# A gMLP and dilated-attention layer on one core: the keys of the stride-16 pattern put in block order where they are made

## The chip, the cores and the metric

The kernel runs on one core of a Trainium2 chip. The metric is the device time of one execution in microseconds (us). A core has a matrix engine (PE, its weight loads shown as PEld), a vector engine (DVE), a scalar engine (ACT), a general engine (POOL) and a queue engine (SP) that issues nearly all transfers here. Each engine works through its own list of instructions in order and waits on semaphores where a result of another engine is needed.

## The reference, cut to what matters

One layer over 2048 tokens of width 1024. A branch A (gated MLP with 128x128 position mixing) and a branch B (attention) are merged by gates and projected. The change touches branch B alone:

```python
DILATED_PATTERNS = ((128, 1), (512, 4), (2048, 16))      # window, dilation
# q, k, v: 16 heads of 64 columns, 2048 tokens
def to_blocks(t):        # L = S // dilation tokens per residue class, blocks of 128
    t = t.reshape(Bn, H, L, dilation, Dh).transpose(0, 1, 3, 2, 4)
    ...
s = jnp.einsum('bhrnqd,bhrnkd->bhrnqk', qb, kw) * (Dh ** -0.5)
...                      # ALiBi penalty, causal window, softmax over s, times v
o = num / sum(alphas)[..., None]       # the three patterns merged by their denominators
```

For dilation 16 there are 16 residue classes of 128 tokens each: query block b holds the tokens b, b+16, b+32 and so on, and attends only to the keys of the same class. The scores of a block are one 128x128 tile.

## The kernel before, in words

All large products are done in two or three parts of split precision: a high part and the rest (`hi`/`lo`, `whi`/`wlo`, `KH`/`KL`, `ph`/`pl`).

**Projections.** The tokens are taken in two halves of 1024 (`hf`), each in two quarters of 512 (`qds`). `unit_S` makes 1024 output columns in four rounds `m` of seven products (a Strassen scheme), with weights cast on ACT (line 83) and their low parts made on POOL (line 86), in a ring of eight tiles. The results of the products go through seven PSUM banks, taken in turn by `bank()`. In each round `evac` is called four times with a 128x512 tile of the result. For k and q that is `ev_qk`: ACT writes `qh` (line 448), DVE writes `ql` (line 449), and two transfers store them in `k_d` or `q_d` in DRAM, in token order. k is made first, then q, in each half.

**Attention.** `window` goes through 16 heads, in each through the patterns p = 2, 1, 0 (dilations 16, 4, 1), and in each pattern through four groups of four query blocks. `load_qk` brings the head's q, KH and KL from DRAM in token order. For p = 2 and p = 1 the columns are put in block order by `permuted`, a generator that is advanced three times per group and that finishes before the pattern it serves: while pattern 0 of head h runs, the keys and queries of pattern 2 of head h+1 are made. For p = 2 these are four copies `QP` on ACT, four `KHP` and four `KLP` on DVE (all line 614), each 128x512 with steps of 16 elements in the input; for p = 1 four `KHP` on DVE and four `KLP` on ACT (line 611).

A group has three stages. `stage_s`: score products (lines 654 and 655, K is the moving operand) into one of two PSUM tiles `ss`, then DVE adds the bias and takes the row minimum (line 662, output `S` and `ob`), then ACT takes the exponential (line 668). `stage_t`, two groups later: PE transposes the probabilities into one of three PSUM tiles `pt` (line 684), ACT writes the high part `ph` (687), DVE the rest `pl` (688). `stage_o`, three groups later: three products per pair with V (lines 701 to 703). After a head's last group `combine` merges its three patterns (DVE, POOL, some PE transposes at line 754), spread over the next head's groups.

Between these stages `run` advances `fill`, 80 units of other projections (line 103, tiles `pj`), so that PE has work while the attention waits. The build then orders the instructions of each engine by its own plan, within the dependences, so the order below is read from the built program.

Of the kernel before, what the change touches and what calls it, by code (L numbers as in the profile page):

```python
# [16 lines left out]
P = 128  # L17
# [10 lines left out]
class Prog:  # L28
# [8 lines left out]
    def setup(self):  # L37
        nc, tc, ctx, io = self.nc, self.tc, self.ctx, self.io
        self.const = c = ctx.enter_context(tc.tile_pool(name="const", bufs=1))
        self.ps = ctx.enter_context(tc.tile_pool(name="ps", bufs=1, space=bass.MemoryType.PSUM))  # L40
        dr = ctx.enter_context(tc.tile_pool(name="dr", bufs=1, space=bass.MemoryType.DRAM))
        self.xp = ctx.enter_context(tc.tile_pool(name="xp", bufs=1))
        self.wk = ctx.enter_context(tc.tile_pool(name="wk", bufs=2))
        self.gn = c.tile([P, KC], F32, name="gn")
        nc.scalar.dma_start(out=self.gn, in_=io["g_norm"])
        self.gv = c.tile([P, KC], F32, name="gv")
        nc.scalar.dma_start(out=self.gv, in_=io["g_v"])
        self.ident = c.tile([P, P], F32, name="ident")
        nc.scalar.dma_start(out=self.ident, in_=io["ident"])
        self.mhalf = c.tile([P, 8], F32, name="mhalf")  # L50
        nc.vector.memset(self.mhalf, -0.5)

        self.gmax = c.tile([P, 1], F32, name="gmax")
        nc.vector.tensor_reduce(out=self.gmax, in_=self.gn, axis=AX.X, op=ALU.max, apply_absolute_value=True)
        self.skq = c.tile([P, 16], F32, name="skq")
        self.sk, self.sq = self.skq[:, 0:8], self.skq[:, 8:16]
        self.sv = c.tile([P, 4], F32, name="sv")
        self.sqk = c.tile([P, 8], F32, name="sqk")
        self.niqk = c.tile([P, 8], F32, name="niqk")
        self.ihv = c.tile([P, 4], F32, name="ihv")  # L60

        self.q_d = [dr.tile([2, P, T], F16, name=f"q_d{i}") for i in range(NH // 2)]
        self.k_d = [dr.tile([2, P, T], F16, name=f"k_d{i}") for i in range(NH // 2)]
        self.v_d = [dr.tile([4, T, 130], F16, name=f"v_d{i}") for i in range(NH // 4)]
        self.ya_d = [dr.tile([D, 512], F32, name=f"ya_d{i}") for i in range(4)]
        self.yb_d = [dr.tile([D, 512], F32, name=f"yb_d{i}") for i in range(4)]
        self.bg_d = [dr.tile([D, 512], F32, name=f"bg_d{i}") for i in range(4)]
        self.ga_d = [dr.tile([D, 512], F32, name=f"ga_d{i}") for i in range(4)]
        self.gb_d = [dr.tile([D, 512], F32, name=f"gb_d{i}") for i in range(4)]
        self.ma_d = [dr.tile([D, 512], F32, name=f"ma_d{i}") for i in range(4)]  # L70
        self.av_d = [dr.tile([T // 2, D], F32, name=f"av_d{i}") for i in range(2)]
        self.o_d = [[dr.tile([T, 66], F32, name=f"o_d{h}_{p}") for p in range(2)] for h in range(NH)]
# [365 lines left out]
                        yield  # L438


    def ev_qk(self, dst, s):
        nc = self.nc

        def ev(nb, qd, ps):
            hi = self.wq.tile([P, 512], F16, name="qh", tag="qh")
            lo = self.wq.tile([P, 512], F16, name="ql", tag="ql")
            sc = s[:, nb:nb + 1]
            nc.scalar.activation(hi, ps, AF.Copy, scale=sc)
            nc.vector.scalar_tensor_tensor(out=lo, in0=ps, scalar=sc, in1=hi, op0=ALU.mult, op1=ALU.subtract)
            for part, t in ((0, hi), (1, lo)):  # L450
                nc.sync.dma_start(out=dst[nb][part][:, 512 * qd:512 * qd + 512], in_=t)
        return ev

    def ev_v(self, vp, hf):
# [41 lines left out]
    def branch_a(self, ap, hf, X):  # L496
        nc, io = self.nc, self.io
        mk = ap.tile([P, P], F32, name="mk", bufs=1)
        nc.sync.dma_start(out=mk, in_=io["causal"])
        ss = ap.tile([P, 8], F32, name="ss", bufs=1)  # L500
        rsv = ap.tile([P, 8], F32, name="rsv", bufs=1)
        nc.vector.tensor_reduce(out=ss, in_=self.ssv, axis=AX.X, op=ALU.add)
        self.rsqrt_mean(rsv, ss, 8)
        um, gr = {}, {}

        def group(g):
            av = ap.tile([P, 8, P], F32, name="avg", tag="avg", bufs=2)
            nc.sync.dma_start(out=av, in_=self.av_d[hf][:, g * P:(g + 1) * P].rearrange("(n p) d -> p n d", p=P))
            nc.vector.tensor_mul(av, av, rsv[:, :, None].broadcast_to([P, 8, P]))
            w = ap.tile([P, P], F32, name="wst", tag="wst")  # L510
            nc.sync.dma_start(out=w, in_=io["wsT"][:, g])
            nc.vector.tensor_mul(w, w, mk)
            b = ap.tile([P, P], F32, name="bsb", tag="bsb")
            nc.sync.dma_start(out=b, in_=io["bs"][:, g])
            return av, w, b

        def ev_u(g, qd, ps):
            q = qd % 2
            av, w, b = gr[g]
            u = um[g, qd] = ap.tile([P, 512], F32, name="um", tag="um", bufs=5)  # L520
            nc.scalar.activation(u, ps, AF.Gelu_apprx_tanh)
            px = self.pt()
            for i in range(4):
                nc.tensor.matmul(px[:, i * P:(i + 1) * P], av[:, 4 * q + i], w, start=True, stop=True)
            m = self.wk.tile([P, 512], F32, name="tm", tag="t5")
            nc.vector.scalar_tensor_tensor(
                out=m.rearrange("p (n t) -> p n t", n=4), in0=px.rearrange("p (n t) -> p n t", n=4),
                scalar=self.gv[:, g:g + 1], in1=b[:, None, :].broadcast_to([P, 4, P]), op0=ALU.mult, op1=ALU.add)
            nc.vector.tensor_mul(u, m, u)

        def ev_g(g, qd, ps):
            t = self.wk.tile([P, 512], F32, name="tg", tag="t5")
            nc.scalar.activation(t, ps, AF.Tanh, scale=0.5)
            nc.vector.scalar_tensor_tensor(out=t, in0=t, scalar=1.0, in1=ps, op0=ALU.add, op1=ALU.mult)
            nc.vector.scalar_tensor_tensor(out=t, in0=t, scalar=0.5, in1=um[g, qd], op0=ALU.mult, op1=ALU.mult)
            nc.sync.dma_start(out=self.ya_d[qd][g * P:(g + 1) * P], in_=t)

        qds = (2 * hf, 2 * hf + 1)
        gu = self.unit_S(X, io["w_in"], 0, ev_u, qds)
        gg = self.unit_S(X, io["w_in"], 2048, ev_g, qds)  # L540
        for g in range(2):
            gr[g] = group(g)
        yield
        for m in range(4):
            yield next(gu)
            for g in (2 * m + 2, 2 * m + 3):
                if g < 8:
                    gr[g] = group(g)
            yield next(gg)
# [66 lines left out]
            yield  # L616
        return r

    def permuted(self, at, raw, p):

        nc = self.nc
        Q, KH, KL = raw[:3]
        k = [Q.rearrange("p (n a q) -> p q n a", q=4, n=4)]
        if p == 2:
            r = yield from self.permute(at, nc.scalar.copy, Q, "QP", p, 1)
            k[0] = r.rearrange("p (b a) -> p b a", a=P)
        k.append((yield from self.permute(at, nc.vector.tensor_copy, KH, "KHP", p, 2)))
        k.append((yield from self.permute(at, nc.vector.tensor_copy if p == 2 else nc.scalar.copy, KL, "KLP", p, 2)))
        self.qkp[p] = k

    def stage_s(self, at, G):
# [14 lines left out]
        for i2 in range(2):  # L646
            ps = self.ps.tile([P, 2, 256], F32, name="ss", tag="ss", bufs=2)
            for i in range(2):
# [2 lines left out]
                n = 256 if prev else P  # L651
                q = Q[:, P * b:P * b + P] if p == 0 else Q[:, b // 4, b % 4] if p == 1 else Q[:, b]
                w = slice(P * (b + 1) - n, P * (b + 1))
                nc.tensor.matmul(ps[:, i, :n], q, KH[:, w], start=True, stop=False)  # L654
                self.pe = nc.tensor.matmul(ps[:, i, :n], q, KL[:, w], start=False, stop=True)  # L655
                rng.append(n)
            for i in range(2):
                j = 2 * i2 + i
# [103 lines left out]
    def window(self, at, fill, total_fill):  # L762
# [26 lines left out]
        for _ in range(24 // self.every * 2):  # L789
            self.seg(fill)  # L790
        raw = {0: self.load_qk(at, 0)}
        for _ in self.permuted(at, raw[0], 2):
            pass
        vt[0, 2] = self.load_v(at, 0, 2)
        for _ in range(24 // self.every * (ahead - 2)):
# [2 lines left out]
        for j in range(n + 3):  # L798
            if j < n:
# [14 lines left out]

                nxt = {2: (h, 1), 0: (h + 1, 2)}.get(p)
                if nxt and nxt[0] < NH and g == 0:
                    perm = self.permuted(at, raw[nxt[0]], nxt[1])
                next(perm, None)
            if 2 <= j < n + 2:
                run(self.stage_t(at, groups[j - 2]))  # L820
# [108 lines left out]
    def run(self):  # L929
# [5 lines left out]
        def drain(g):  # L935
            for _ in g:
                pass
# [4 lines left out]
        with pool("tp", bufs=1) as self.tp, pool("wr", bufs=2) as self.wr, pool("cp", bufs=1) as self.cp:  # L942
            X = [None, None]
            for hf in range(2):
# [27 lines left out]
                with pool(f"wq{hf}", bufs=2) as self.wq:  # L972
                    branch_a = self.branch_a(self.wq, hf, X)
                    next(branch_a)
                    for c0, dst, sc in ((4096, self.k_d, self.sk), (3072, self.q_d, self.sq)):
                        drain(self.unit_S(X, win, c0, self.ev_qk(dst, sc), qds))
                    drain(branch_a)
                if hf == 0:
                    drain(self.unit_S(X, win, 6144, self.ev_bg, qds))
# [70 lines left out]
```

## Time and profile before

| | us |
|---|---|
| median of 3 runs | 2652.31 (2652.05 to 2658.41) |
| the profiled execution | 2664.8, span of its instructions 2663.0 |
| PE busy in the span | 2497.5 |
| DVE busy | 1835.0 |
| ACT busy | 1261.1 |
| POOL busy | 886.1 |

The mean granted clock of PE in the profiled execution is 0.982 of full speed. Three stages matter here. k is made from 245 to 327 us (first half of the tokens) and from about 1000 to 1085 us (second half). The attention window runs from about 1335 to 2285 us. After it comes a final projection. A matmul's shown duration includes its way through the array: matmuls overlap, so PE's busy time is longer than its work and its idle time is shorter than what it lost.

### The profile page before, as it was taken

What the parts mean: (1) busy time and instruction counts of PE and PEld (TensorE: products, weight loads), DVE (VectorE), ACT (ScalarE), POOL (GpSimd) and SP (SyncE); (2) the same over time, 40 slices, a digit from 0 to 9 for tenths busy, and PEclk for the clock granted to TensorE, in tenths of its full rate; (3) what the DMA queues carried; (4) which work ended last, traced back from release to release, by engine and by line L of the source; (5) the groups of instructions that cost most, each with busy time, mean ns of one, the idle gap of its engine ahead of it and who ended that gap; (6) DMA issues with size and microseconds to landing.
All of it is one profiled execution on the core that took longest, in us unless ns stands there. A gap on an engine that the chain in (4) does not pass through costs nothing. (4 is left out here: it accounts for less than half of the span.)

```text
span 2663.0 us, 45389 instructions
## 1 busy us (share of the span) xinstructions
PE 2497.5 (94%) x16736; PEld 2112.4 (79%) x16736; DVE 1835.0 (69%) x3777; ACT 1261.1 (47%) x2577; POOL 886.1 (33%) x633
## 2 busy tenths in 40 slices
PE   5969999999998899999999999999989898899998
PEld 5969888888887898888778788777777776677787
DVE  5764767755347646687768888798989888544533
ACT  4235333343333354333267777776767665222311
POOL 0335544445444345544322222333433332000000
PEclk9989999999999999999999999999999999999999
DMA  7744333343444333333266656676777875855531
GB/s 230 165 125 140 107 122 104 99 162 123 136 161 103 83 121 122 121 103 118 73 182 167 185 147 174 178 212 189 212 221 200 230 215 165 252 171 174 177 128 64
DMA packets 463998, 410.03 MB, mean 154 GB/s; under 512 B 150432, under 2 KB 384288, under 8 KB 463776
## 3 DMA queue, kind: packets, MB, share of 16 engines
q1 hardware_dynamic: 463344, 407.05, 52.2%
q8 instruction: 132, 2.16, 0.4%
q14 instruction: 90, 0.74, 0.1%
q10 hardware_dynamic: 432, 0.07, 0.0%
HBM read 297.35 MB, written 109.71 MB: 153 GB/s over the span
## 5 line engine op out<-in xcount | busy, mean ns | idle before, releaser
L103 PE MATMUL pj<-X,whi 128*128 128x512 f32 x1792 | 597.1, 408 | 6.6 <-DVE gb L891 5.1
L86 POOL TENSOR_TENSOR wc<-wraw,wc 128x512 fp32r<-128x512 f32 x240 | 327.5, 1373 | 322.7 <-ACT wc L83 316.1
L103 PEld LDWEIGHTS pj<-X,whi 128*128 128x128 f32 x1792 | 339.6, 193 | 76.9 <-ACT whi L83 6.9
L103 PE MATMUL pj<-X,wlo 128*128 128x512 f32 x896 | 366.5, 409 | 5.8 <-DVE wlo L86 3.0
L662 DVE CUSTOM_DVE_ANT_0 S<-ss,B,niqk 128x256 f32<-128x256 f32 (+1 forms) x768 | 283.3, 418 | 14.4 <-PE ss L655 14.2
L688 DVE SCALAR_TENSOR_TENSOR pl<-pt,ph 128x512 f16<-128x512 f32 x320 | 204.8, 652 | 74.4 <-ACT ph L687 73.5
L668 ACT ACTIVATE S<-S,ob 128x128 f32<-128x128 f32 (+1 forms) x512 | 194.5, 437 | 73.9 <-DVE ob L662 73.3
L83 ACT CAST wc<-wraw 128x512 fp32r<-128x512 f32 x240 | 144.5, 617 | 151.6 <-PE pt L103 71.1
L85 POOL TENSOR_SCALAR whi<-wraw 128x1024 fp32r<-128x1024 f32 x64 | 72.9, 1139 | 416.0 <-PE pj L103 387.3
L103 PEld LDWEIGHTS pj<-X,wlo 128*128 128x128 f32 x896 | 173.2, 193 | 43.0 <-DVE wlo L86 5.5
L687 ACT ACTIVATE ph<-pt 128x512 f16<-128x512 f32 x320 | 176.5, 563 | 47.3 <-PE pt L684 28.5
L103 PE MATMUL pt<-X,wc 128*128 128x512 f32 x768 | 189.6, 395 | 0.0
L103 PE MATMUL ss<-T,wc 128*128 128x512 f32 x768 | 187.6, 393 | 0.0
L103 PE MATMUL pj<-WO,X 128*128 128x512 f32 x768 | 181.2, 396 | 3.3 <-ACT X L892 3.1
L684 PE MATMUL pt<-ident,S 128*128 128x128 f32 x1200 | 168.4, 276 | 14.1 <-DVE pl L688 14.0
L103 PEld LDWEIGHTS pj<-WO,X 128*128 128x128 f32 x768 | 143.9, 188 | 40.0 <-ACT X L892 4.4
L103 PEld LDWEIGHTS pt<-X,wc 128*128 128x128 f32 x768 | 144.0, 188 | 34.0
L86 POOL TENSOR_TENSOR wcl<-wraw,wch 128x1024 fp32r<-128x1024 f32 x52 | 129.2, 2486 | 124.6 <-ACT wch L83 103.6
L103 PEld LDWEIGHTS ss<-T,wc 128*128 128x128 f32 x768 | 143.6, 188 | 32.0
L86 POOL TENSOR_TENSOR wlo<-wraw,whi 128x1024 fp32r<-128x1024 f32 x64 | 163.1, 2548 | 5.3
L103 PE MATMUL pt<-T,wc 128*128 128x512 f32 x672 | 162.9, 391 | 0.0
L684 PEld LDWEIGHTS pt<-ident,S 128*128 128x128 f32 x1200 | 138.9, 142 | 28.7 <-DVE pl L688 18.3
(230 smaller groups left out, 5828.0 us busy)
## 6 DMA issues: line engine op xcount, KB each, us to landing
wraw<-in_w_in SPq DMA_DIRECT2D x64, 1024.0 KB, 5.8
V<-v_d SPq DMA_DIRECT2D x48, 520.0 KB, 4.8
o_d<-ob SPq DMA_DIRECT2D x32, 528.0 KB, 4.7
OC<-o_d SPq DMA_DIRECT2D x32, 528.0 KB, 5.2
wraw<-in_w_in SPq DMA_DIRECT2D x32, 512.0 KB, 5.0
wraw<-in_w_proj_a SPq DMA_DIRECT2D x32, 512.0 KB, 5.3
wraw<-in_w_proj_b SPq DMA_DIRECT2D x32, 512.0 KB, 4.5
xt<-in_xT SPq DMA_DIRECT2D x60, 256.0 KB, 4.6
```

The lines of the kernel that those rows point to most:

```text
L83: nc.scalar.copy(hi, raw)
L85: nc.gpsimd.tensor_scalar(out=hi, in0=raw, scalar1=1.0, scalar2=0.0, op0=ALU.mult, op1=ALU.add)
L86: self.w_lo.tensor_tensor(out=lo, in0=raw, in1=hi.bitcast(F32), op=ALU.subtract)
L103: self.pe = nc.tensor.matmul(out, st(a, k), mv(b, k), start=first and n == 0, stop=last and n == len(todo) - 1)
L662: nc.vector.tensor_tensor_reduce(out=S[:, j, :n], in0=ps[:, i, :n], in1=B[:, bo:bo + n], scale=self.niqk[:, pr:pr + 1], scalar=3e38, op0=A ...
L668: nc.scalar.activation(S[:, i, :rng[i]], S[:, i, :rng[i]], AF.Exp, bias=ob[:, i, 65:66], scale=-1.0)
L684: self.pe = nc.tensor.transpose(px[:, j * P:(j + 1) * P], G["S"][:, i, c * P:(c + 1) * P], self.ident)
L687: nc.scalar.activation(ph[:, :n], px[:, :n], AF.Copy, scale=PSCALE)
L688: nc.vector.scalar_tensor_tensor(out=pl[:, :n], in0=px[:, :n], scalar=PSCALE, in1=ph[:, :n], op0=ALU.mult, op1=ALU.subtract)
```

## The change

In `ev_qk`, for k alone, each 128x512 part is copied once more into a tile `qp` in the order "class, then token", the high part on ACT and the rest on DVE, and stored in a new DRAM tensor `kp_d`. A pool of two `qp` tiles serves both parts. In the attention, pattern 2 no longer copies KH and KL: it loads KHP and KLP from `kp_d` with four transfers of 64x2048 per head. Since each quarter of the tokens is permuted by itself, a block's 128 keys now lie in four pieces of 32, 512 elements apart, and the score products of pattern 2 read K, and write `ss`, through that shape. The pool of `um` tiles in branch A goes from five to four.

```diff
+        self.kp_d = [dr.tile([2, P, T], F16, name=f"kp_d{i}") for i in range(NH // 2)]
...
-    def ev_qk(self, dst, s):
+    def ev_qk(self, dst, s, perm=None):
...
             for part, t in ((0, hi), (1, lo)):
                 nc.sync.dma_start(out=dst[nb][part][:, 512 * qd:512 * qd + 512], in_=t)
+                if perm is not None:
+                    r = self.wq.tile([P, 16, 32], F16, name="qp", tag="qp", bufs=2)
+                    (nc.vector.tensor_copy if part else nc.scalar.copy)(r, t.rearrange("p (a q) -> p q a", q=16))
+                    nc.sync.dma_start(out=perm[nb][part][:, 512 * qd:512 * qd + 512],
+                                      in_=r.rearrange("p q a -> p (q a)"))
...
-            u = um[g, qd] = ap.tile([P, 512], F32, name="um", tag="um", bufs=5)
+            u = um[g, qd] = ap.tile([P, 512], F32, name="um", tag="um", bufs=4)
...
-    def permuted(self, at, raw, p):
+    def permuted(self, at, raw, h, p):
...
         if p == 2:
+            rr = slice(64 * (h % 2), 64 * (h % 2) + 64)
+            for part, name in ((0, "KHP"), (1, "KLP")):
+                t = at.tile([P, T], F16, name=name, tag=name, bufs=2)
+                for j in range(2):
+                    nc.sync.dma_start(out=t[64 * j:64 * j + 64], in_=self.kp_d[h // 2][part][rr])
+                k.append(t.rearrange("p (c q a) -> p q c a", c=4, q=16))
             r = yield from self.permute(at, nc.scalar.copy, Q, "QP", p, 1)
             k[0] = r.rearrange("p (b a) -> p b a", a=P)
-        k.append((yield from self.permute(at, nc.vector.tensor_copy, KH, "KHP", p, 2)))
-        k.append((yield from self.permute(at, nc.vector.tensor_copy if p == 2 else nc.scalar.copy, KL, "KLP", p, 2)))
+        else:
+            k.append((yield from self.permute(at, nc.vector.tensor_copy, KH, "KHP", p, 2)))
+            k.append((yield from self.permute(at, nc.scalar.copy, KL, "KLP", p, 2)))
...
-                nc.tensor.matmul(ps[:, i, :n], q, KH[:, w], start=True, stop=False)
-                self.pe = nc.tensor.matmul(ps[:, i, :n], q, KL[:, w], start=False, stop=True)
+                o, kh, kl = ((ps[:, i, :n].rearrange("p (c a) -> p c a", c=4), KH[:, b], KL[:, b]) if p == 2 else
+                             (ps[:, i, :n], KH[:, w], KL[:, w]))
+                nc.tensor.matmul(o, q, kh, start=True, stop=False)
+                self.pe = nc.tensor.matmul(o, q, kl, start=False, stop=True)
```

PE's order of instructions is the same before and after. DVE's, ACT's and SP's change at the places of the copies and transfers, and in the attention window DVE takes other copies into the room. Three places follow.

DVE at the start of pattern 0 of a head in the middle of the window, before (`KHP<-KH` of line 614 is the copy for pattern 2 of the next head, `S,OC` the bias step of pattern 0):

```order
L688 SCALAR_TENSOR_TENSOR pl<-pt,ph 128x512
L747 TENSOR_TENSOR cb<-OC 128x4x64
L614 COPY KHP<-KH 128x512 x2
L688 SCALAR_TENSOR_TENSOR pl<-pt,ph 128x384
L662 ISA S,OC<-ss,B,niqk 128x128
L662 ISA OC 128x1
```

DVE at the same place, after (lines have moved by some; `KHP<-KH` of line 617 is the copy for pattern 1 of the next head):

```order
L763 TENSOR_TENSOR cb<-OC 128x4x64
L704 SCALAR_TENSOR_TENSOR pl<-pt,ph 128x512
L617 COPY KHP<-KH 128x512 x4
L678 ISA S,OC<-ss,B,niqk 128x128
L678 ISA OC 128x1
L704 SCALAR_TENSOR_TENSOR pl<-pt,ph 128x384
```

The two copies for pattern 2 are gone, and all four copies for pattern 1, which stood later, now stand ahead of the first bias step of pattern 0.

DVE one group later in the same head, before:

```order
L662 ISA S,OC<-ss,B,niqk 128x256
L662 ISA OC 128x1
L688 SCALAR_TENSOR_TENSOR pl<-pt,ph 128x512
L614 COPY KLP<-KL 128x512 x4
L611 COPY KHP<-KH 128x512
L688 SCALAR_TENSOR_TENSOR pl<-pt,ph 128x384
L758 TENSOR_TENSOR yb<-pt,sbg 128x512
L611 COPY KHP<-KH 128x512 x3
```

DVE there, after:

```order
L678 ISA S,OC<-ss,B,niqk 128x256
L678 ISA OC 128x1
L704 SCALAR_TENSOR_TENSOR pl<-pt,ph 128x512
L704 SCALAR_TENSOR_TENSOR pl<-pt,ph 128x384
L774 TENSOR_TENSOR yb<-pt,sbg 128x512
```

The two `pl` steps, which free two `pt` tiles for PE, stood five copies apart and now follow each other.

DVE in one round of k's projection, from the fourth product's result on, before (`c` and `u_...` are tiles of results, `wraw_...` sums of weights for the next round):

```order
L375 TENSOR_TENSOR c<-pj,u_2854 128x512
L375 TENSOR_TENSOR u_2804<-pj,u_2804 128x512
L449 SCALAR_TENSOR_TENSOR ql<-c,skq,qh 128x512
L375 TENSOR_TENSOR u_2854<-pt,u_2854 128x512
L449 SCALAR_TENSOR_TENSOR ql<-u_2854,skq,qh 128x512
L375 TENSOR_TENSOR u_2804<-ss,u_2804 128x512
L360 TENSOR_TENSOR wraw_3086<-s_3094,wraw_3086 128x4x128
L449 SCALAR_TENSOR_TENSOR ql<-u_2804,skq,qh 128x512
L362 TENSOR_TENSOR wraw_3086<-wraw_3086 128x4x128
```

DVE in such a round, after:

```order
L376 TENSOR_TENSOR c<-pj,u_3095 128x512
L376 TENSOR_TENSOR u_3039<-pj,u_3039 128x512
L450 SCALAR_TENSOR_TENSOR ql<-c,skq,qh 128x512
L455 COPY qp<-ql 128x512
L376 TENSOR_TENSOR u_3095<-pt,u_3095 128x512
L450 SCALAR_TENSOR_TENSOR ql<-u_3095,skq,qh 128x512
L455 COPY qp<-ql 128x512
L376 TENSOR_TENSOR u_3039<-ss,u_3039 128x512
L361 TENSOR_TENSOR wraw_3345<-s_3353,wraw_3345 128x4x128
L450 SCALAR_TENSOR_TENSOR ql<-u_3039,skq,qh 128x512
L363 TENSOR_TENSOR wraw_3345<-wraw_3345 128x4x128
```

A `qp` copy has come behind the first two `ql` (that of the third stands some rows later), among steps that evacuate PSUM and prepare weights. Each waits until the store of the `qp` tile before last has landed.

More of the change, by code (lines that the diff above doesn't have):

```diff
@@ L791, in window @@
         raw = {0: self.load_qk(at, 0)}
-        for _ in self.permuted(at, raw[0], 2):
+        for _ in self.permuted(at, raw[0], 0, 2):
             pass
@@ L816, in window @@
                 if nxt and nxt[0] < NH and g == 0:
-                    perm = self.permuted(at, raw[nxt[0]], nxt[1])
+                    perm = self.permuted(at, raw[nxt[0]], *nxt)
                 next(perm, None)
@@ L975, in run @@
                     for c0, dst, sc in ((4096, self.k_d, self.sk), (3072, self.q_d, self.sq)):
-                        drain(self.unit_S(X, win, c0, self.ev_qk(dst, sc), qds))
+                        drain(self.unit_S(X, win, c0, self.ev_qk(dst, sc, self.kp_d if c0 == 4096 else None), qds))
                     drain(branch_a)
```

## The prediction

> **What bounds the kernel now.** I read the page, then a table of stages, then what PE waits for, then the chain, then single stretches of the timeline. The table of stages first (PE, PEld, DVE, ACT and POOL busy us, the granted clock, the DMA share): the two rounds in which k is made, and the attention window.
>
> ```profile
> 245.00:327.00 82.00, 82.00 (x358) 66.82 (x357) 56.16 (x68) 29.03 (x49) 39.83 (x29) 1.00 0.38 123
> 1000.00:1080.00 80.00, 80.00 (x349) 65.09 (x348) 52.04 (x62) 30.75 (x61) 40.87 (x30) 1.00 0.39 123
> 1360.00:2240.00 880.00, 812.11 (x7986) 681.33 (x7984) 768.99 (x2373) 638.27 (x1477) 271.84 (x191) 0.98 0.70 192
> ```
>
> While k is made PE never stops, and DVE has 26 of 82 us free. In the window PE is idle for 880.0 - 812.1 = 67.9 us, DVE is busy for 769.0 of 880 us (87%). PE is still the bound there, but DVE is close behind it, and what PE loses, it loses to DVE. The waits of PE that belong to the attention, over the whole run (total us, times, longest):
>
> ```profile
> PE ss L654 <- DVE ob L662: 35.1, 72, 2.6
> PE pt L684 <- DVE pl L688: 14.0, 14, 2.9
> PE po L703 <- DVE pl L688: 9.2, 13, 2.6
> PE po L701 <- ACT ob L704: 6.6, 10, 1.8
> ```
>
> The work that the change takes from DVE is in the groups by shape (busy us, mean ns), and the range of one copy in the view of its line:
>
> ```profile
> L614 DVE COPY KLP<-KL 128x512 f16<-128x512 f16 x64 | 54.5, 903 | 0.0
> L614 DVE COPY KHP<-KH 128x512 f16<-128x512 f16 x64 | 50.0, 797 | 4.7 <-DMA KH<-k_d 4.7
> L611 DVE COPY KHP<-KH 128x512 f16<-128x512 f16 x64 | 29.7, 502 | 0.0
> L614 ACT COPY QP<-Q 128x512 f16<-128x512 f16 x64 | 74.0, 1186 | 5.6 <-DMA bg_d<-tbg 4.4 <-DMA Q<-q_d 1.1
> ...
> L614 DVE COPY KLP<-KL x64: 601/654/2894, 1349.6 to 2178.2; 128x512 f16<-128x512 f16 x64
> ```
>
> So 54.5 + 50.0 = 104.5 us leave DVE, nearly all in the window: its share there falls to about three quarters. How much of that is time depends on how often PE stands behind such a copy. One episode, DVE and then PE (start us, duration):
>
> ```profile
> 1708.68 0.70 DVE L688 SCALAR_TENSOR_TENSOR pl<-pt,ph 128x512 f16<-128x512 f32 x1
> 1709.29 4.27 DVE L614 COPY KLP<-KL 128x512 f16<-128x512 f16 x4
> 1713.45 0.44 DVE L611 COPY KHP<-KH 128x512 f16<-128x512 f16 x1
> 1713.79 0.57 DVE L688 SCALAR_TENSOR_TENSOR pl<-pt,ph 128x384 f16<-128x384 f32 x1
> ...
> 1714.41 0.55 PE L684 MATMUL pt<-ident,S 128*128 128x128 f32 x3 [2.08 <-DVE pl L688]
> ...
> 1830.98 0.68 PE L684 MATMUL pt<-ident,S 128*128 128x128 f32 x3 [2.11 <-DVE pl L688]
> ```
>
> PE has filled all three `pt` tiles and stands for 2.08 us until `pl` frees one, and `pl` stood behind four copies (4.27 us). The last row is the same case two heads later. A stall has a second price, which the table of stages shows just behind these two:
>
> ```profile
> 1715.20:1718.60 3.40, 3.40 (x21) 2.82 (x17) 2.98 (x12) 2.20 (x6) 0.00 (x0) 0.50 0.53 154
> 1831.20:1834.60 3.40, 3.40 (x29) 2.95 (x28) 3.35 (x13) 2.65 (x7) 0.00 (x0) 0.51 0.64 185
> ```
>
> For 3.4 us PE got half its clock, so each such stall loses another 1.7 us.
>
> **The change, part by part.**
>
> *The DVE copies of pattern 2 go.* PE can gain only what it waits for. The wait that carries the copies is that of `pt` for `pl`, 14.0 us, since the order puts KLP directly ahead of `pl`. Its longest, 2.9 us, is not theirs:
>
> ```profile
> 2080.61 2.62 DVE L145 TENSOR_TENSOR X<-xl,X 128x512 fp32r<-128x512 f32 x1 [2.64 <-ACT X L144]
> ...
> 2083.89 1.12 PE L684 MATMUL pt<-ident,S 128*128 128x128 f32 x4 [2.91 <-DVE pl L688]
> ```
>
> There DVE waited for a loaded tile of the fill and then split it. That leaves 14.0 - 2.9 = 11.1 us, which I credit in full: the freed 4.27 us of the episode is twice the wait. The other two waits for DVE, 35.1 us on `ob` and 9.2 us of `po` on `pl`, I leave: 23.1 us of the first stand ahead of pattern 1's scores (the rows below), and there the order has no copy of pattern 2 but the merging of the head before. Bounds for the part: 0, if all waits only move on to the next late thing, and 14.0 + 35.1 + 9.2 = 58.3 us, if a lighter DVE is never late. I stay near the low end, since the row is that of the episode.
>
> ```profile
> L654 PE MATMUL ss<-KHP,Q 128*128 128x256 f16 x192 | 47.8, 275 | 12.3 <-DVE ob L662 12.0
> L654 PE MATMUL ss<-KHP,Q 128*128 128x128 f16 x64 | 14.2, 221 | 11.1 <-DVE ob L662 11.1
> ```
>
> *The half clock.* Two stretches behind copies, 2 x 1.7 = 3.4 us more. The Trainium skill ("TensorE: Matmul & The Clock Gate", section "Why this matters for your kernels") asks for idle gaps of about 3 us or more before the clock is halved. Here 2.08 and 2.11 us were enough, so trace and page differ, and I keep the row; by the page the sum would be 3.4 us smaller.
>
> *What DVE's order gives back.* The four KHP copies of pattern 1 (502 ns each) now stand together ahead of the first bias step of pattern 0, 4 x 0.50 = 2.0 us, where two copies of line 614 stood, 2 x 0.61 = 1.2 us by the 1.22 us that they took in the episode's head. Pattern 0's first scores come up to 0.8 us later, in the six heads that the order shows with four together: at most 5 us. PE has fill to do at that place, so I take 2 us; bounds 0 and 5.
>
> ```profile
> 1705.61 1.22 DVE L614 COPY KHP<-KH 128x512 f16<-128x512 f16 x2
> ```
>
> *The copies where k is made.* 32 evacuations, two copies each: 32 on ACT at the price of QP, which has the same steps, 32 x 1.19 = 38 us; 32 on DVE at the 0.65 us of KLP's median, or 0.90 us at its mean, 21 to 29 us. Per half that is 11 to 15 us of DVE work in a stage with 26 us free, and 19 us of ACT in one with 53 us free. PE's row there is 82.00 of 82, and seven PSUM banks stand between PE and the evacuation. A product takes PE 2.69 us (a round of seven repeats every 286.37 - 267.53 = 18.84 us), so DVE and ACT may fall up to 7 x 2.69 = 18.8 us behind before PE stops. Cost 0 if that cover holds; the third rival prices its loss.
>
> ```profile
> 267.53 1.76 DVE L362 TENSOR_TENSOR wraw<-wraw 128x512 f32<-128x512 f32 x1 [2.60 <-POOL wc L86]
> 286.37 1.76 DVE L362 TENSOR_TENSOR wraw<-wraw 128x512 f32<-128x512 f32 x1 [2.60 <-POOL wc L86]
> ```
>
> A rule speaks against these copies. The rows first:
>
> ```profile
> 1349.57 5.55 DVE L614 COPY KLP<-KL 128x512 f16<-128x512 f16 x4
> 1350.67 2.74 POOL L86 TENSOR_TENSOR wlo<-wraw,whi 128x1024 fp32r<-128x1024 f32 x1
> ```
>
> Four KLP copies took 5.55 us while POOL split weights, where four at the median take 2.6. The Trainium skill ("SBUF — State Buffer", section "Who interferes with whom") says that a DVE copy in a fast mode and a POOL operation lock each other out of one pair of ports, whole instructions long; the trace agrees. In k's stage POOL is busy for 39.83 of 82 us, so by that rule half of the 16 DVE copies per half would wait for a POOL operation, and the DVE time would be nearer the mean than the median. Either value lies under the cover, so the sum does not change.
>
> *Transfers.* 64 stores of 128 KB where k is made, 64 loads of 256 KB in the window, 16.8 MB on top of 167.5 MB there:
>
> ```profile
> q1 hardware_dynamic: 215754, 167.49, 68.9%
> ...
> KH<-k_d SPq DMA_DIRECT2D x28, 256.0 KB, 5.5
> ...
> DVE mn L723 <- DMA OC<-o_d: 16.0, 13, 3.2
> ```
>
> The share would rise by 68.9% x 16.8 / 167.5 = 6.9 points. A load lands in about 5.5 us. The order issues it behind SP's loads of B and V for pattern 1 and ahead of the next weights, so about pattern 0's length before it is needed (a head takes 880 / 16 = 55 us, a pattern some 18). I take 0. Bounds: 0, and a tenth more on the one transfer for which DVE waits, 1.6 us. The `pattern 2` keys now wait for their transfer, and PE's first score of pattern 2 stands behind that wait; with 18 us in hand for 5.5 it costs nothing.
>
> *The score products of pattern 2.* K is read in four pieces of 32 columns. No row shows a moving operand in pieces. The nearest rows are the weight loads of contiguous QP and of Q, half of which are read in steps of four elements:
>
> ```profile
> L654 PEld LDWEIGHTS <-Q 128*128 128x128 f16 x512 | 52.9, 105 | 9.0 <-issue 6.9
> L654 PEld LDWEIGHTS <-QP 128*128 128x128 f16 x256 | 24.4, 98 | 1.4 <-issue 1.4
> ```
>
> 7 ns on the mean, at most 14 ns for a stepped one; on 512 products 0 to 7 us. I take 0, as runs of 32 are far nearer to contiguous. `um` with four tiles: a tile is needed again seven products (18.8 us) after the step that frees it, so nothing.
>
> Sum: -11.1 - 3.4 + 2 = -12.5 us. The profiled execution (2664.8) becomes 2652.3. It lies 12.5 us above the median of the runs (2652.3), so against that median the forecast is 2639.8, rounded 2640 us.
>
> **The rivals.**
>
> *The gain is larger.* A DVE at 75% is less often late everywhere, and the 35.1 us of short waits on `ob` (72 of them, 0.5 us each) shrink too. For it: the copies of pattern 1 move to earlier places. Against it: in pattern 1 the merging stays, line by line. With half of the 58.3 us and the 3.4 us of clock, less 2: 2652.3 - 30.6 = 2622.
>
> *The waits only move.* PE's order is fixed, and behind `pl` stands ACT's `ph`, behind `ob` the merging; a stall taken away at one place is met at the next. For it: DVE's waits for ACT.
>
> ```profile
> L688 DVE SCALAR_TENSOR_TENSOR pl<-pt,ph 128x512 f16<-128x512 f32 x320 | 204.8, 652 | 74.4 <-ACT ph L687 73.5
> ```
>
> DVE often has nothing to do before `pl` but wait for ACT (73.5 us), so speed on DVE need not reach PE. A third of the 14.5 us credited and 2 given back leave -2.8: 2649.5.
>
> *k's stage becomes the bound: slower than before.* Of the two `qp` tiles one holds the high part and one the rest, so an evacuation cannot copy before the last one's store has landed. The landings of k's stores in one round, the burst of three and then the fourth:
>
> ```profile
> L451 SPq DMA_DIRECT2D k_d<-qh x3: 319/320/531, 278.3 to 282.7; - x3
> DMA to landing us min/median/max: 1.7/4.1/5.7
> ...
> DMA to landing us min/median/max: 1.7/1.7/1.8
> ```
>
> A turn of a tile is copy 1.19 + issue 0.32 + landing L, and there are 18.84 / 4 = 4.71 us for each, so DVE and ACT fall behind from L = 3.2 us on. Taking the burst's three values and the fourth's 1.7, the average is 3.3: the edge. With twice the stores and L = 5.7 throughout, the lag over 16 evacuations is 16 x (5.7 + 1.51 - 4.71) = 40 us, 21 beyond the cover of 18.8, in each half: +42 - 12.5 = +30, 2682 us. It decides the sign from 2 x (16 (L - 3.2) - 18.8) = 12.5, L = 4.8 us. Against it: after k comes q without such copies, and the burst is followed by a pause of a third of the round.
>
> **How the numbers follow.** No change means within 0.3%, 8 us, about what a measurement of this kernel can tell. The forecast (a gain of 8 to 22 us) gets 0.47, the larger gain 0.16, the waits that only move (within 8 us) 0.25, the slower k stage 0.12. So faster 0.63, same 0.25, slower 0.12. The range goes from beyond the larger gain, 2614, to just above no change, 2658, and leaves out most of the slower case and a tail of the larger gain, 2 in 10; the likeliest case alone would be 2630 to 2644.
>
> **What the profile after would show.** Right: no line of KLP or KHP copies of pattern 2 on DVE, DVE near 670 us of the window, the wait of `pt` for `pl` at some 3 us, fewer stretches at half clock, the window about 12 us shorter, k's stage at its 18.84 us per round. Wrong: PE gaps in k's stage with ACT or DVE waiting for `kp_d` stores; `ss` waiting longer for `ob` at the start of pattern 0; the products of pattern 2 longer than before; DVE or PE waiting for KHP loads.

## The result

| | before | after |
|---|---|---|
| median, same chip | 2655.36 us (2652.05 to 2660.28, 4 runs) | 2672.0 us (2670.67 to 2673.24, 4 runs) |
| ratio to before | 1 | 1.0061, 95% interval 1.0040 to 1.0082 |
| span of the profiled execution | 2663.0 us | 2671.0 us |
| mean granted clock | 0.982 | 0.985 |

The changed kernel is slower by 0.61%, about 16 us. It was forecast at 2640 us with a range of 2614 to 2658.

The table of stages of the kernel after, for the same three stretches (PE, PEld, DVE, ACT and POOL busy us, granted clock, DMA share):

```profile
245.00:327.00 82.00, 78.48 (x338) 62.92 (x337) 58.15 (x73) 40.57 (x55) 34.40 (x25) 1.00 0.44 139
1000.00:1080.00 80.00, 79.53 (x377) 65.95 (x377) 51.33 (x66) 43.72 (x78) 36.15 (x27) 1.00 0.45 142
1360.00:2240.00 880.00, 822.49 (x8001) 689.07 (x8000) 687.93 (x2242) 639.00 (x1475) 267.08 (x194) 0.99 0.80 214
```

The window did what was forecast: DVE's share falls from 769.0 to 687.9 us, and PE is idle for 57.5 us instead of 67.9. In the first stretch, where PE had never stood still, it now issues 338 matmuls instead of 358. PE's waits over the whole run (total us, times, longest):

```profile
PE ss L670 <- DVE ob L678: 24.8, 49, 2.9
...
PE pt L104 <- DVE u L376: 10.3, 8, 2.1
...
PE po L717 <- ACT ob L720: 7.2, 11, 1.8
PE pt L700 <- DVE pl L704: 6.2, 4, 3.9
```

The attention's waits for DVE fell (35.1 to 24.8 and 14.0 to 6.2 us). A new one is there, of a projection's product (line 104) for an addition on DVE (line 376), in the stages that make k and q and in branch A behind them.

How late PE is against the kernel before, at the same product, tells where the time went. PE's order is the same in all these kernels, so this is the start of one product minus its start before (worked out from the PE rows of both traces):

| us later than before, PE | k begins | q ends | in branch A |
|---|---|---|---|
| first half of the tokens | -2.3 | 3.9 | 10.9 |
| second half | 8.5 | 15.7 | 22.4 |

k and q cost 6.1 and 7.2 us, branch A, where nothing was edited but the number of `um` tiles, 7.1 and 6.7 us: 27.1 us. The window then gives back 14.4 us (22.4 to 8.0 us behind it). Between the halves the profiled execution of the kernel before lost 2 to 8 us that the others don't lose, so the halves are counted apart. That is also why its span is only 8 us shorter than that of after, where the medians differ by 16.6 us.

### The profile page after: what moved, and what is told of

Its sections match the earlier page's. It is cut to its first block, busy times and chain, and to the rows that moved or that the text cites. A ratio compares the mean times of both kernels' runs of the same rounds, so it can differ in the third digit from the quotient of the medians.

```text
span 2671.0 us, 45587 instructions
## 1 busy us (share of the span) xinstructions
PE 2493.5 (93%) x16736; PEld 2102.0 (79%) x16736; DVE 1784.5 (67%) x3681; ACT 1292.7 (48%) x2609; POOL 873.5 (33%) x633
## 3 DMA queue, kind: packets, MB, share of 16 engines
q8 instruction: 132, 2.16, 0.4%
## 4 chain that ended last, share of the span: by engine, by line
PE 32%; DVE 9%; DMA 7%; ACT 5%; issue 3%; POOL 2%; SPq 0%; DVEq 0%; POOLq 0%; ACTq 0%
PE pj L104 21%; DVE S L678 3%; PE pt L700 2%; PE pt L104 2%; DMA OC<-o_d 2%; ACT S L684 2%; DMA o_d<-ob 1%; DVE pl L704 1%; PE ss L104 1%; ACT QP L620 1%; POOL wc L87 1%; DMA wraw<-in_w_proj_b 1%; PE ss L670 1%; DVE OC L758 1%; PE ss L671 1%
## 5 line engine op out<-in xcount | busy, mean ns | idle before, releaser
L104 PEld LDWEIGHTS pj<-X,wlo 128*128 128x128 f32 x896 | 171.5, 191 | 51.0 <-POOL wlo L87 10.9
L104 PE MATMUL pt<-T,wc 128*128 128x512 f32 x672 | 163.6, 392 | 10.4 <-DVE u L376 10.3
L104 PEld LDWEIGHTS pt<-T,wc 128*128 128x128 f32 x672 | 125.3, 188 | 40.2 <-issue 11.8
L87 POOL TENSOR_TENSOR wlo<-wraw,whi 128x1024 fp32r<-128x1024 f32 x64 | 154.6, 2416 | 5.1
```

Of the source, the lines that this page charges most:

```text
L87: self.w_lo.tensor_tensor(out=lo, in0=raw, in1=hi.bitcast(F32), op=ALU.subtract)
L104: self.pe = nc.tensor.matmul(out, st(a, k), mv(b, k), start=first and n == 0, stop=last and n == len(todo) - 1)
```

## How k's stage loses time

PE's rows of the kernel before: the fourth product of a round, and that of the next round. Then the second product of a round, and the addition on DVE that reads it:

```profile
264.59 2.88 PE L103 MATMUL pt<-T,wc 128*128 128x512 f32 x12
...
283.95 2.88 PE L103 MATMUL pt<-T,wc 128*128 128x512 f32 x12
```

```profile
278.42 2.96 PE L103 MATMUL pt<-X,wc 128*128 128x512 f32 x12
...
288.05 0.68 DVE L375 TENSOR_TENSOR c<-pt,u 128x512 f32<-128x512 f32 x1
```

PE's round is 283.95 - 264.59 = 19.36 us, 2.77 us per product. The 18.84 us in the prediction is the round of DVE. So DVE and ACT are not paced by PE. They run behind it, 288.05 - (278.42 + 2.96) = 6.7 us here. This lag is 2.5 us in k's first round, where it grows, and from the second on DVE and ACT catch up 0.5 us per round: 7.2, 6.7, 6.2, 5.6, 5.1, 4.6, 4.0 us in the rounds of k and q that follow, and 3.5 us in the first of branch A. 18.84 us is what a loop takes that goes through the engines in turn: an addition on DVE, the evacuation `qh` and the weight casts on ACT, their low parts on POOL, the weight differences on DVE, the next addition. No engine on it is full, and yet it has 0.5 us per round in hand. Where it runs through ACT, before and after:

```profile
277.52 0.72 ACT L448 ACTIVATE qh<-c,skq 128x512 f16<-128x512 f32 x1 [5.31 <-DVE c L375]
278.15 0.61 ACT L83 CAST wc<-wraw 128x512 fp32r<-128x512 f32 x1
```

```profile
280.06 0.72 ACT L449 ACTIVATE qh<-c,skq 128x512 f16<-128x512 f32 x1 [5.84 <-DVE c L376]
280.81 1.18 ACT L455 COPY qp<-qh 128x512 f16<-128x512 f16 x1
281.90 0.62 ACT L84 CAST wc<-wraw 128x512 fp32r<-128x512 f32 x1
...
290.37 1.21 ACT L455 COPY qp<-qh 128x512 f16<-128x512 f16 x1 [0.95 <-DMA kp_d<-qp]
291.48 0.62 ACT L84 CAST wc<-wraw 128x512 fp32r<-128x512 f32 x1
```

Behind 5.8 us in which ACT had nothing to do, the copy takes the place ahead of the cast for which POOL waits. The second one also waits 0.95 us for a store. The same addition on DVE in two rounds of k, after:

```profile
267.73 0.71 DVE L376 TENSOR_TENSOR c<-pt,u 128x512 f32<-128x512 f32 x1
...
292.00 0.68 DVE L376 TENSOR_TENSOR c<-pt,u 128x512 f32<-128x512 f32 x1
```

DVE's round is now 24.27 us, against 18.84 us before and PE's 19.36. So the lag grows, 8.0, 12.9, 17.4 us in k's second to fourth round and 18.5 us in q's first, until a bank is not free when PE comes back to it:

```profile
316.68 3.02 PE L104 MATMUL pt<-X,wc 128*128 128x512 f32 x12 [1.23 <-DVE c L376]
...
324.67 3.01 PE L104 MATMUL pt<-T,wc 128*128 128x512 f32 x12 [2.13 <-DVE u L376]
```

While PE stands, the lag falls with it, to 13.2 us in q's third round. After that it falls by 0.5 us per round only, and is 12.1 us in the first round of branch A instead of 3.5. Branch A has its own products of line 530 in the `pt` banks, and there PE pays for the lag (PE's waits from 345 to 600 us in the trace of after, total us, times, longest):

```profile
PE pt L530 <- DVE c L376: 2.6, 1, 2.6
PE pt L530 <- DVE u L376: 2.1, 2, 1.2
PE pt L104 <- DVE u L376: 1.0, 1, 1.0
```

These are 5.7 us, and behind the longest of them the trace's record of the clock has 3.4 us at half clock, 1.7 us more.

That was read from two traces. The runs below test it: what part each half of the change has, whether it is copies or stores, and whether it is the amount of work or its place.

## The experiments

Each ratio is to the kernel before on the same chip, with its 95% interval. It is the ratio on record, which can differ from the quotient of the two medians by up to 0.15%, 4 us.

**The copies alone.** The loads and score products of the attention are those of the kernel before.

```diff
-            for part, name in ((0, "KHP"), (1, "KLP")): ...          # loads from kp_d
+        k.append((yield from self.permute(at, nc.vector.tensor_copy, KH, "KHP", p, 2)))
+        k.append((yield from self.permute(at, nc.vector.tensor_copy if p == 2 else ..., KL, "KLP", p, 2)))
```

> The half of the change that lies where k is made, alone: the copies into block order and their stores are kept, and the attention loads and permutes the keys itself as the kernel before does (the stored block order is read by nobody). Theory of the chain: the copies lie on a loop of ACT, POOL and DVE that turns once in a round of seven products and had no slack (18.84 us before, the same as PE's seven products), so each round of k is some 3 us longer, the loss is never made good, and this kernel is 25 to 32 us over the kernel before. Theory of the landing (a copy waits until the store that read its tile has landed): the same total, since the stores are here too. Rival, that the extra time is made in the attention (pieces of the score products, later loads): no more than 5 us over the kernel before.

Measured: 2683.85 us against 2659.14, ratio 1.0106 (1.0083 to 1.0130). The loss is all in this half. The expectation still took 18.84 us for PE's round; with 19.36 us the loop has 0.5 us in hand, not nothing. PE lost 4.8 + 6.4 us in the first half and 6.8 + 7.9 us in the second, 25.8 us; over the window its delay stays as it was (19.8 us ahead of it, 19.1 behind).

**The attention alone.** The pool of `um` tiles is back at five.

```diff
-                    nc.sync.dma_start(out=t[64 * j:64 * j + 64], in_=self.kp_d[h // 2][part][rr])
+                    nc.sync.dma_start(out=t[64 * j:64 * j + 64], in_=self.k_d[h // 2][part][rr])
...
-                        ... self.ev_qk(dst, sc, self.kp_d if c0 == 4096 else None) ...
+                        ... self.ev_qk(dst, sc) ...
```

> The other half alone: nothing is copied or stored in block order where k is made, and the attention loads its keys for the stride-16 pattern, and reads them in pieces, as the changed kernel does, but from the stored keys in token order. Left out is therefore the permutation of the keys of that pattern; the instructions of the attention and their order are those of the changed kernel. Theory of the chain, and my prediction's term for the attention: 12 to 16 us under the kernel before. Rival, that the attention gains nothing and the change lost only there or in both: within 4 us of the kernel before, or above it.

Measured: 2644.78 us against 2659.14, ratio 0.9947 (0.9927 to 0.9967), so 14 us. The two halves together make -14.4 + 24.7 = +10 us, and the whole change +16.

**More tiles.**

```diff
-                    r = self.wq.tile([P, 16, 32], F16, name="qp", tag="qp", bufs=2)
+                    r = self.wk.tile([P, 2, 16, 32], F16, name="qp", tag="t5" if part else "ld",
+                                     **({} if part else {"bufs": 3}))[:, 0]
```

> The changed kernel with more tiles for the copies in block order: three for the high part and two for the rest, instead of two for both. Theory of the landing: the copies no longer wait for the store that read their tile, and 20 us or more of the 30 us lost where k is made come back, so that the kernel is at 2640 to 2652 us, level with or under the kernel before. Theory of the chain: only the few waits on the loop go (some 0.4 us in a round on DVE, less on ACT), 3 to 6 us in all, and the kernel stays 10 to 15 us over the kernel before.

Measured: 2665.02 us against 2659.14, ratio 1.0036 (1.0018 to 1.0054). The waits for stores in the first half, of after and then of this kernel (idle us before the copies, times):

```profile
  DMA kp_d<-qp: 10.0, 12
```

```profile
  DMA kp_d<-qp: 3.1, 1
```

PE's loss falls from 27.1 to 20.1 us. The landing of the stores has 7 us of it and not 20. Neither theory gave the time: +5.9 us (9.6 by the ratio) is above the one and under the 10 to 15 us of the other.

**No stores.** The copies alone, without this:

```diff
-                    nc.sync.dma_start(out=perm[nb][part][:, 512 * qd:512 * qd + 512],
-                                      in_=r.rearrange("p q a -> p (q a)"))
```

> The half where k is made, alone, and without the stores of the copies: both copies into block order are made and then dropped, so nothing waits for a landing and no byte more is moved; the attention is as in the kernel before. Theory of the chain: the copies' own durations on the loop remain (1.2 us on ACT and 0.65 us on DVE, some 2.2 to 2.6 us in a round), and the kernel is 18 to 27 us over the kernel before. Theory of the landing or of the added transfers: within 5 us of the kernel before.

Measured: 2675.46 us, ratio 1.0076 (1.0053 to 1.0099), +16 us (20 by the ratio), at the low end of what I expected; by PE's delay 20.4 of the 25.8 us remain with no byte stored. Both tests say much the same: 5 to 7 us for the stores by PE's delay (8 us by the medians of this pair), some 20 us for the copies themselves.

**One copy alone, on ACT and on DVE.**

```diff
-                if perm is not None:
+                if perm is not None and part == 0:      # the second kernel: part == 1
```

> The half where k is made, with the copy and the store of the high part alone (on ACT); the rest is neither copied nor stored in block order, and the attention is as in the kernel before. Theory of the chain: each copy on ACT (1.2 us, four in a round) delays the loop only where it stands ahead of a cast or an evacuation that the loop waits for, some 1.2 to 1.5 us in a round, so 10 to 15 us over the kernel before; this and the next run together give the 25 us of both copies. Rival, that the cost is one of transfers or of the waits for landings: half of the 8 us that the stores cost so far, 4 us.

> The half where k is made, with the copy and the store of the rest alone (on DVE); the high part is neither copied nor stored in block order, and the attention is as in the kernel before. Theory of the chain: two or three of the four copies of a round (0.65 us each) stand between sums and evacuations that follow each other on the loop, some 1.3 us in a round, so 9 to 14 us over the kernel before. Rival, that DVE had room for them (26 of 82 us idle): within 4 us of the kernel before.

Measured: ACT's copy alone 2676.74 us against 2656.76, ratio 1.0075 (1.0053 to 1.0097); DVE's alone 2684.03 us, ratio 1.0101 (1.0081 to 1.0121). Both missed my numbers: 20 us instead of 10 to 15, and 27 instead of 9 to 14. The two don't add up to 25, each costs nearly as much as both. By PE's delay (table below) they cost 3.2 and 8.3 us in k and q, and both together 11.6; what each pays in full is branch A, 16.9 and 14.5 us against 14.3 for both. The lag left there in the first half is nearly the same in the three runs, 12.4 and 12.1 us against 11.5. DVE's round in k grows from 18.8 to 21.4 us with ACT's copy and to 22.3 us with DVE's. Two rows of each trace show why DVE's copy costs more than its 0.67 us, DVE and then POOL; with DVE's copy alone:

```profile
281.62 1.63 DVE L455 COPY qp<-ql 128x512 f16<-128x512 f16 x1
...
281.38 1.34 POOL L87 TENSOR_TENSOR wc<-wraw,wc 128x512 fp32r<-128x512 f32 x1 [3.29 <-ACT wc L84]
```

With both copies and no stores:

```profile
280.63 0.67 DVE L455 COPY qp<-ql 128x512 f16<-128x512 f16 x1
...
281.66 1.29 POOL L87 TENSOR_TENSOR wc<-wraw,wc 128x512 fp32r<-128x512 f32 x1 [4.54 <-ACT wc L84]
```

Without ACT's copy the cast comes earlier, POOL's split starts just ahead of DVE's copy, and the copy takes 1.63 us instead of 0.67. Of the 32 copies 25 start while POOL splits and take 1.17 to 1.74 us, the other seven 0.64 to 0.68 us. With ACT's copy the cast and POOL come later (POOL waits 4.54 us for the cast instead of 3.29), and the two don't meet. So ACT's copy delays the loop on one side while it spares DVE's copy a collision on the other. By the Trainium skill ("SBUF — State Buffer", section "Who interferes with whom") DVE's fast copy and POOL lock each other out of shared ports for a whole instruction; the two pairs of rows agree with it.

**The same copies in other places.** Three `qh` and `ql` tiles, five tiles in turn for the copies with one store for both parts, and an order by hand: each copy is queued on its engine behind a cast or a difference of a later round.

```diff
+            if perm is not None:
+                todo.append((nb, qd, act, hi, lo))
+                if len(todo) > 2:
+                    flush()                 # the copies of two evacuations ago
...
+                on = (nc.vector.tensor_copy if i % 4 else nc.scalar.copy) if part else nc.scalar.copy
...
+            for k, w_ in ((1, a), (2, a), (3, b)):      # a, b: casts of the 3rd and 6th weight of a round
+                self.behind((r - 3, k), w_, d)          # d: the difference a11 = s1 - a11 on DVE
+            self.behind((r - 2, 0), b)
```

> The changed kernel, whole, with the same copies held back to the places where the loop leaves ACT and DVE waiting: on ACT five in a round (the high parts, and one of the rests), two behind a cast ahead of the 3.28 us wait and three ahead of the 5.31 us wait; on DVE three, behind the difference of line 360 of the kernel before, ahead of the 2.60 us wait for POOL. Each evacuation's two parts share one tile and one store, five tiles in turn, three tiles each for the evacuated parts. Theory of the chain: it is the place and not the amount of work that costs, k's rounds are back at about 18.84 us, and the whole kernel is 10 to 16 us under the kernel before. Rival, that the amount of added work costs (more ACT and DVE time, contention with POOL, more transfers): no better than with more tiles, 5 to 15 us over the kernel before.

Measured: 2643.91 us against 2656.76, ratio 0.9956 (0.9937 to 0.9975). This version is under both kernels. ACT, where three of its five copies lie, and DVE:

```profile
289.49 2.30 ACT L474 COPY qp<-qh 128x512 f16<-128x512 f16 x2
291.70 1.20 ACT L474 COPY qp<-ql 128x512 f16<-128x512 f16 x1
293.95 0.72 ACT L458 ACTIVATE qh<-c,skq 128x512 f16<-128x512 f32 x1 [1.06 <-DVE c L385]
```

```profile
299.94 1.25 DVE L474 COPY qp<-ql 128x512 f16<-128x512 f16 x2
302.63 1.76 DVE L366 TENSOR_TENSOR wraw<-wraw 128x512 f32<-128x512 f32 x1 [1.44 <-POOL wc L88]
```

Ahead of `qh` ACT still has 1.06 us left of 5.31, ahead of the weight difference DVE 1.44 of 2.60. The stage's row and PE's work are those of the kernel before, with 22 us more on ACT and 10 more on DVE:

```profile
245.00:327.00 82.00, 82.00 (x358) 66.82 (x357) 66.25 (x81) 51.48 (x70) 43.61 (x31) 1.00 0.54 170
```

PE's delay does not change through k, q and branch A in either half (-0.7 and -8.5 us throughout). DVE's round in k is 18.7 us. So it is the place of the copies that costs, not their amount, nor the bytes stored. To hold the copies back took more tiles and half as many stores, so the place alone was not run; more tiles in the old place gave back 7 of the 27 us.

**Copies in two rounds of four.** The copies alone, for the first two rounds of k (the other keys are not stored in block order).

```diff
-                if perm is not None:
+                if perm is not None and nb < 4:
```

> The half where k is made, with the copies and stores of both parts in the first two of k's four rounds alone; the other two rounds copy and store nothing in block order, and the attention is as in the kernel before. Theory of the chain: the lag of the evacuation behind PE, about 7 us at k's start, rises by 4 to 5 us in each of the two rounds, to about 13 to 16 us, which stays within the cover, so PE does not stop while k and q are made. After that it falls by only 0.5 us in a round (18.84 against PE's 19.37), so that 10 to 13 us are left where branch A begins, and PE stands there for 4 to 6 us in each half: 8 to 13 us over the kernel before, all of it lost after 390 us and after 1160 us. Rival, that the stage recovers once the copies end (two rounds of k and four of q): lag back at 3.5 us at branch A, within 3 us of the kernel before.

Measured: 2664.63 us against 2660.82, ratio 1.0023 (1.0010 to 1.0036). The time is under what I expected (+4 us, at most 10, for 8 to 13), and the copies raised the lag in one round alone, from 6.6 in k's second round to 11.7 us in its third; where PE stands is as expected. Its waits from 245 to 600 us are all those of branch A:

```profile
PE pt L530 <- DVE u L376: 2.8, 1, 2.8
PE pt L530 <- DVE c L376: 0.2, 1, 0.2
```

The lag then falls, 11.2, 10.7, 10.1, 9.6, 9.1, 8.5 us, half a microsecond per round, and 8.5 us are left for branch A, where PE's delay rises by 5.0 us (5.1 in the second half); in k and q it does not rise at all. That a lag is handed on to a stage two units later, and costs time there, is so shown by itself.

PE's loss in all runs, from the starts of the same products (us, both halves of the tokens), beside the difference of the medians:

| kernel | in k and q | in branch A | sum | medians, whole kernel |
|---|---|---|---|---|
| after | 6.1 + 7.2 | 7.1 + 6.7 | 27.1 | +16.6 |
| copies alone | 4.8 + 6.8 | 6.4 + 7.9 | 25.8 | +24.7 |
| the same without stores | 2.4 + 3.3 | 7.0 + 7.8 | 20.4 | +16.3 |
| ACT's copy alone | 1.3 + 1.9 | 10.1 + 6.8 | 20.0 | +20.0 |
| DVE's copy alone | 3.6 + 4.7 | 7.0 + 7.5 | 22.7 | +27.3 |
| two rounds of four | 0 + 0 | 5.0 + 5.1 | 10.2 | +3.8 |
| after, more tiles | 2.3 + 3.6 | 7.5 + 6.7 | 20.1 | +5.9 |
| after, other places | 0 + 0 | 0 + 0 | 0 | -12.9 |
| attention alone | 0 + 0 | 0 + 0 | 0 | -14.4 |

The last column has the attention's gain in it in the first and the last three rows. Sum and median agree within about 6 us, which is about the scatter of single runs.

## Why the prediction was wrong

*The copies where k is made, priced at 0.* This is the step that failed: it measured 27.1 us by PE's delay in the changed kernel (24.7 us by the medians of the copies alone). Its pieces, one by one. The round of 18.84 us was read from DVE's rows and called PE's; PE's is 19.36 us, and the difference, 0.5 us, was all that DVE and ACT had in hand. The cover was counted as whole, 18.8 us; about 7 us of it were in use from k's second round on without any copy, and what is taken is given back at 0.5 us per round, so that branch A pays for what q has not given back. The free time on DVE (26 us) and ACT (53 us) was counted as room for the copies; it was time in which the loop waited, and a copy that stands ahead of the next instruction of the loop lengthens it. That PE's row was at 82.00 of 82 showed that the cover had not run out, not how much was left.

*The third rival*, that k's stage becomes the bound, had the right sign and place, and the wrong mechanism for the most part: the stores' landing is 5 to 7 us of the 27, and 20 us remain when nothing is stored. It got 0.12.

*The attention*, forecast at -12.5 us, gave -14.4 us in the run by itself. The terms behind the sum were less good than the sum: the wait of `pt` for `pl`, credited with 11.1 us, fell by 7.8; that of `ss` for `ob`, which I left at nothing, fell by 10.3, of which 3.6 came back as waits for `OC`, which the same bias step writes (1.1 to 4.7); that of `po` for `pl` fell from 9.2 to 4.8. The 2 us that the order was to give back don't show: `ss` of pattern 0 waits 9.1 us in all instead of 10.5. That the sum came within 2 us is in part luck.

*The half clock*, 3.4 us: both stretches went, and others came elsewhere. By the trace's record of the clock the window has nine stretches before and six after, and what they lose is 17.1 and 15.4 us. In the version with the copies in other places it is 22.2 us, the likely reason why its window gains less than that of the attention alone.

*The transfers* and *the score products in pieces*, both 0, held. The products of pattern 2, and the loads:

```profile
L670 PE MATMUL ss<-KHP,QP 128*128 128x128 f16 x256 | 37.0, 220 | 2.9 <-DVE ob L678 0.6 <-DVE OC L678 0.3
```

```profile
KHP<-kp_d SPq DMA_DIRECT2D x32, 256.0 KB, 6.4
```

220 ns per product, against 219 ns for the same products before; a load lands in 6.4 us and PE waits for none. The DMA share rose from 0.70 to 0.80, not by 6.9 points, and DVE waited 21.8 us for `OC` instead of 16.0, which is 5.8 us more where the bound was 1.6, with no cost seen on PE. At the window's start DVE stands once for 9.9 us, put down to a load of KHP; with the attention alone it stands there for 10.4 us, put down to ACT, and PE goes on in both.

*`um` with four tiles*, 0: the copies in other places run with four, and branch A costs nothing there.

## What to carry to other kernels

Idle time of an engine is room only if something else than a chain of results ends it. Measure the period of each engine's rounds separately, and the lag of the consumer behind the producer round by round: if it shrinks by 0.5 us in a round of 19.4, then 0.5 us is the room, whatever the busy shares say. If work must be added there, queue it behind the instruction that feeds the loop and ahead of the longest wait; a lag that a buffer covers is paid at the next place with less cover.

## What the hardware showed

The DVE copy of 128x512 took 0.64 to 0.69 us in the run with both copies and no stores, where none started while POOL was splitting, and 1.63 us where it started 0.24 us behind a split of 1.34 us. A copy of 1.2 us on a third engine, ACT, decided which.

A stall of PE of about 2.1 us does not always halve its clock. With the copies alone, a stall of 2.16 us in k's stage is followed by 3.4 us at half clock, and a product of 4.57 us instead of 2.9; in the changed kernel a stall of 2.13 us at the same place is followed by one of 3.01 us:

```profile
324.99 4.57 PE L104 MATMUL pt<-T,wc 128*128 128x512 f32 x12 [2.16 <-DVE u L376]
329.40 2.91 PE L104 MATMUL pj<-T,wc 128*128 128x512 f32 x12
```

Over all ten traces (from 200 us on, without the last 60) 23 of 34 stalls between 2.0 and 2.25 us that began at full clock were followed by half clock, which set in before the end of the stall or within 2.5 us of it. What decides it is open; the prediction counted 1.7 us for each such stall.
